# A trunk of one retention layer and one attention layer on one core: norm row spread by products with ones, sample rows handled last, program order in the output projection

## The chip, the cores and the metric

The kernel runs on one NeuronCore of one Trainium2 chip, as one program for the whole inference step. The metric is device time in microseconds (us) of one execution, the median of three runs. Names of engines: PE is the tensor engine (PEld its weight loads), DVE the vector engine, ACT the scalar engine, POOL the GpSimd engine, SP the engine that only issues transfers; ACT issues transfers too.

## The reference, cut to what matters

Two layers, first retention, then sliding-window attention, on 1024 prompt tokens and on 8 sample ("decode") tokens, each of 1024 features. All numbers are fp32.

```python
def rmsnorm(x, g):
    y = x * rsqrt(mean(x * x, -1) + EPS); return y * g

# layer 0, retention: h = rmsnorm(x, norm_ret); q, k, v, gate = split(h @ w_in_ret)
#   o = chunkwise recurrent retention, also the new state;  o = rmsnorm(o, ret_out_norm) * silu(gate)
#   x = x + o @ w_out_ret
# layer 1, attention: h = rmsnorm(x, norm_swa); q, k, v, gate = split(h @ w_in_swa)
#   q = rmsnorm(q, q_norm); k = rmsnorm(k, k_norm)          # per head of 64
#   p = softmax over a 128-token window, with one sink column per head and a linear bias
#   o = (p @ v) * silu(gate);  x = x + o @ w_out_swa
```

Outputs are both token sets after the trunk, the retention states and the last window of keys and values. The sample tokens attend to 128 cached keys each.

## The kernel before, in words

PE works nearly all the time on products in which each fp32 operand is split into a high and a low part, and three products (high by high, high by low, low by high) are summed in PSUM. So almost every operand passes through a pair of operations first: a copy to the high part on ACT, and a subtraction that gives the low part on DVE or POOL. The order of PE's instructions is the order in which the code issues them, throughout. On the other engines there are two regimes. In the first stage (everything inside the stack `se`) and in the first part of the attention layer (`sk`), `manual_schedule` names ACT, DVE, POOL and SP too, and they run in program order. After `sk.close()` (attention proper and the output projection), a scheduler in the compiler orders these four engines by its own estimates.

**The start (lines 382 to 502 and 861 to 898).** The prompt comes in chunks of 128 tokens, `X[0]` to `X[7]`; `X[8]` is the 8 sample rows. `xload(c)` loads a chunk on SP's queue. `sq(c)` makes the sum of squares on ACT (line 431), `pw(c)` the power -1/2 of the mean on POOL (lines 435 and 120), `sc(c)` multiplies the chunk by that and by the norm row `gb` on DVE (line 440), `TR(c, b)` transposes the eight 128 by 128 blocks of it on PE (line 105) into two PSUM banks, and `hi` and `lo` (457 and 461) split the transposed blocks into the operands `xh` and `xl`. `gb` is the vector `norm_ret` on all 128 partitions: one transfer that reads the row 128 times, 512 KB, on ACT's queue (line 866). The sample rows are transposed into `p8` (tile `pd`), copied to `rdec`, and `dcols` (495 and 496) puts two of their columns behind each 256 token columns of `xh` and `xl`. `w_hi` and `w_lo` (221 and 226) split the weights. The first products are plain ones (line 544, in slots of 24 matmuls); the first slot reads the columns of chunk 0, chunk 2 and the sample rows, and the third slot begins with the transposes of chunk 1. Between the first two slots' weight splits (on POOL) and those transposes lie `pw(1)` on POOL and `sc(1)` on DVE.

**The attention's last turns (lines 2360 to 2395).** 64 units (head pair by chunk) go through scores (`att_s`, 1988 to 1992), normalisation (`att_r`, 1999 and 2000), transposes (`att_x`) and the product with values (`att_o`, 2022; `att_out`, 2036). For the last head pair, `att_out` writes the operand of the output projection itself: the high part on ACT (line 2044), the low part on DVE (line 2045), into `SA`. From unit 58 on, `fill` mixes in products of the output projection.

**The output projection (`so_all`, from line 2189).** 24 products (8 feature tiles by 3 token ranges) of 24 matmuls each (lines 1660 to 1662) rotate over three PSUM tiles. `finish` adds the residual on DVE (2232), `so_y` transposes on DVE (2164), and four transfers on ACT's queue write the result; residual tiles `xr` (two buffers) are loaded on SP's queue (2220, 2222) when one is free; `so_ahead` loads and splits the next weight slot (1646, 1649, 1650). The third token range has the sample columns as well.

**The decode attention,** mixed into these products. `dec_scores` first computes the factor `r16` of the sample queries (tile `r`: lines 2068 to 2070 and 2072 on DVE, and the power on POOL, line 120 of `rsq`), then scores, softmax over 16 rows by 1032 columns (2081 to 2097, with an exponential on ACT, 2092). `dec_pt` transposes the result and builds `PTd` (ACT, 2109) and the masked `M8` (DVE, 2110; tile `pm`). `dec_o` multiplies with the values (2122, 2124), copies to `god` (tile `gdec`, ACT, 2128), multiplies by the gate (2130) and writes the sample columns of `SA`, high (2131) and low (2132).

Of the kernel before, what the change touches and what calls it, by code (L numbers as in the profile page):

```python
# [7 lines left out]
F32 = mybir.dt.float32  # L8
F32R = mybir.dt.float32r
AF = mybir.ActivationFunctionType  # L10
ALU = mybir.AluOpType
# [3 lines left out]
D = 1024  # L15
NP = 1024
# [8 lines left out]
HD = 64  # L25
# [45 lines left out]
def _trunk(ctx, tc, nc, a):  # L71
# [343 lines left out]
    X, SS, PO = {}, {}, {}  # L415

    def xload(c):
        if c in (0, 1, 2, 3):
            X[c] = xq.tile([128, D], F32, tag="xq", bufs=4, name="xq")
        elif c == 7:  # L420
            X[c] = raw_tile()
        else:
            X[c] = sp.tile([128, D], F32, tag="u", bufs=3, name="u")
        if c == 8:
            X[c] = X[c][0:ND, :]
        nc.sync.dma_start(out=X[c], in_=x_sample[:, 0, :] if c == 8 else x_prompt[0, c * 128:c * 128 + 128, :])
# [436 lines left out]
    for r in range(2):  # L863
        pool.memset(oneh[:, r, r:r + 1], 1.0)
    pool.memset(rdec32, 0.0)
    nc.scalar.dma_start(out=gb, in_=norm_ret[0].partition_broadcast(128))
    nc.scalar.dma_start(out=ident, in_=a["c1"][:, 0:128])
    act(warm, warm, AF.Silu)
    for c in (0, 8, 2):
        xload(c)  # L870
# [5 lines left out]
        raw_load(k0, r, nc.sync)  # L876
    for c in (4, 6, 7):
        xload(c)
    for c in (8, 0, 2):
        sq(c)  # L880
        pw(c)
    sc(8)
    p8 = vdp.tile([128, 8, ND], F32, tag="vd", name="pd8")
    for k in range(8):
        tr(p8[:, k, :], X[8][:, k * 128:k * 128 + 128], ident[:ND, :ND])
    sc(0)
    TR(0, 1)
    dve.tensor_copy(rdec, p8)
    sc(2)
    TR(2, 2)  # L890
    dcols(0, B11)
    dcols(0, B21)
    for c, name in ((0, "A11"), (2, "A12")):
        for j in range(2):
            hi(c, j)
            lo(c, j)
        w_hi(q0, name, 0)
        w_lo(q0, name, 0, pool)
    ev.sort(key=lambda e: e[:2])
    for n, s in enumerate(slots):  # L900
        while pes and pes[0][0] <= s.t:
# [1160 lines left out]

    dd = {}

    def dec_scores():

        rr = rbc[0:16, NP:NT]
        nc.vector.tensor_tensor(r16, ms16, rr, ALU.mult)
        nc.vector.tensor_tensor(r16, r16, rr, ALU.mult)
        nc.vector.tensor_scalar(r16, r16, 1.0 / HD, EPS, ALU.mult, ALU.add)  # L2070
        rsq(r16, r16, 8)
        nc.vector.tensor_tensor(r16, r16, rr, ALU.mult)
        ddec = atp.tile([16, 129], F32, tag="s", name="ddec", bufs=6)
        nc.sync.dma_start(out=ddec, in_=a["c2"][0:16, c2w() - 129:])
        S16 = rbc[0:16, :].rearrange("p (b s) -> p b s", b=8)
        for hf in range(2):
            psc = scp.tile([128, 512], F32, tag="sc", name="sc")
            for i in range(4):
                b = 4 * hf + i
                mm(psc[:16, i * 128:i * 128 + 128], Qd[:, :, b], kcT["t"][:, b, :], start=True, stop=True)  # L2080
            nc.vector.tensor_tensor(S16[:, 4 * hf:4 * hf + 4, 0:128], psc[:16, :].rearrange("p (b s) -> p b s", b=4),
                                    r16[:, 4 * hf:4 * hf + 4].unsqueeze(2).broadcast_to([16, 4, 128]), ALU.mult)
        pn = trp.tile([128, 512], F32, name="tr")
        for b in range(8):
            mm(pn[:16, b:b + 1], Qd[:, :, b], kdT[:, b:b + 1], start=True, stop=True)
        nc.vector.tensor_tensor(S16[:, :, 128], pn[:16, 0:8], r16, ALU.mult)
        nc.vector.tensor_tensor(S16, S16, ddec.unsqueeze(1).broadcast_to([16, 8, 129]), ALU.add)
        nc.vector.tensor_reduce(m16, S16, mybir.AxisListType.X, ALU.max)
        nc.vector.tensor_scalar(m16, m16, skc, None, ALU.max)
        nc.vector.tensor_tensor(S16, S16, m16.unsqueeze(2).broadcast_to([16, 8, 129]), ALU.subtract)  # L2090
        S16f = rbc[0:16, :]
        nc.scalar.activation(S16f, S16f, AF.Exp)
        nc.scalar.activation(e16, m16, AF.Exp, scale=-1.0, bias=skc)
        nc.vector.tensor_reduce(t16, S16, mybir.AxisListType.X, ALU.add)
        nc.vector.tensor_tensor(t16, t16, e16, ALU.add)
        nc.vector.reciprocal(t16, t16)
        nc.vector.tensor_tensor(S16, S16, t16.unsqueeze(2).broadcast_to([16, 8, 129]), ALU.mult)
        dd["S"] = S16
# [253 lines left out]
    for m in range(0, NU, 2):  # L2352
        if m == 50:
            so_ahead(1)
        if m == 56:
            drain(ps)
            so_ahead(2)
        if m == 58:
            so_ahead(3)
            src = out  # L2360
        reloads(m)
        sc_(m + L)
        fill(src, W)
        sc_(m + L + 1)
        fill(src, W)
        if m % 4 == 2:
            us = units[m - 2:m + 2]
            for u in us:
                until(G, (u.p, u.ti))
            att_o(us)  # L2370
        fill(src, 2 * W)
        for n_ in (2, 3):
            if m + n_ < NU:
                att_x(units[m + n_])
            fill(src, W)
        att_split()
        reloads(m)
    reloads(NU)
    fill(out, 6.0)
    assert not held & {4, 5}  # L2380
    dec_scores()
    dec_vload()
    fill(out, 14.0)
# [43 lines left out]
```

## Time and profile before

| quantity | us |
|---|---|
| median of three runs | 1290.34 (1289.12 to 1291.25) |
| the profiled execution's own time | 1292.0 |
| its span on the core | 1290.2 |
| PE busy in the span | 1263.0 (98%) |

The page gives the busy time of each engine, windows give it for stretches of the span together with the granted clock of PE (1.00 is full speed) and the transfers' rate, the list of waits says which instruction of which line released a waiting one, and the timeline lists instructions in order of time, with the idle time ahead of them in brackets. All times are counted from the span's start. What lies between span and time of the execution is 1.8 us here.

### The profile page before, as it was taken

To read this page: it belongs to the slowest core of one execution; us is meant where nothing else is said; L and a number is where in the kernel's file an instruction comes from. 1 tells how busy PE (TensorE), PEld (TensorE's weight loads), DVE (VectorE), ACT (ScalarE), POOL (GpSimd) and SP (SyncE) were. 2 spreads that over 40 slices of the span, in tenths; PEclk is the share of its full clock that TensorE was granted. 3 is DMA by queue.
4 is the path that set the end of the run, shared out by engine and by line. 5 is a ranking of instruction groups with operands and counts; after the bars stand their busy time and mean duration, and the time that the engine had idled before them with its cause. 6 is when DMAs were issued, how large, how long until landed. Compare 5 with 4: busy or idle time off the path is not lost.

```text
span 1290.2 us, 26727 instructions
## 1 busy us (share of the span) xinstructions
PE 1263.0 (98%) x9780; PEld 1210.0 (94%) x9780; DVE 778.8 (60%) x1512; ACT 647.7 (50%) x1570; POOL 730.6 (57%) x838
## 2 busy tenths in 40 slices
PE   6999999999999999999999999999999999998998
PEld 5999999999999999988889999999999999998988
DVE  5954656665575764476774656764667666765422
ACT  5533445454555554588771234545566655663010
POOL 5654444535359899798771457726465655654010
PEclk9999999999999999999999999999999999999989
DMA  6313867687668683556879855943031222237434
GB/s 227 108 54 120 252 186 233 182 253 216 189 208 229 189 243 103 184 173 204 264 209 258 234 188 159 276 118 103 19 114 50 66 67 67 66 111 241 85 75 86
DMA packets 245679, 206.68 MB, mean 160 GB/s; under 512 B 63992, under 2 KB 220532, under 8 KB 245532
## 3 DMA queue, kind: packets, MB, share of 16 engines
q1 hardware_dynamic: 189840, 170.61, 44.0%
q10 hardware_dynamic: 55708, 34.37, 9.1%
q8 instruction: 77, 1.26, 0.4%
q14 instruction: 54, 0.44, 0.1%
HBM read 135.41 MB, written 70.55 MB: 160 GB/s over the span
## 4 chain that ended last, share of the span: by engine, by line
PE 88%; DVE 4%; DMA 2%; ACT 2%; POOL 2%; issue 1%; SPq 0%; ACTq 0%; DVEq 0%; POOLq 0%
PE b L335 8%; PE b L336 8%; PE b L337 8%; PE S L1302 7%; PE pj L1660 6%; PE pj L1661 5%; PE pj L1662 5%; PE b L328 4%; PE b L329 4%; PE b L330 4%; PE tr L105 4%; PE o L2022 2%; PE b L544 1%; PE S L335 1%; PE S L336 1%
## 5 line engine op out<-in xcount | busy, mean ns | idle before, releaser
L335 PE MATMUL b<-xh,woh 128*128 128x258 f32 x784 | 223.2, 285 | 0.0
L337 PE MATMUL b<-xh,wol 128*128 128x258 f32 x784 | 221.7, 283 | 0.0
L336 PE MATMUL b<-xl,woh 128*128 128x258 f32 x784 | 221.6, 283 | 0.0
L1660 PE MATMUL pj<-SA,wh 128*128 128x384 f32 (+1 forms) x496 | 168.5, 340 | 2.2 <-DVE qs L1876 0.8
L1661 PE MATMUL pj<-SA,wh 128*128 128x384 f32 (+1 forms) x496 | 159.1, 321 | 2.8 <-DVE SA L2045 2.5
L1662 PE MATMUL pj<-SA,wl 128*128 128x384 f32 (+1 forms) x496 | 159.0, 321 | 0.0
L335 PEld LDWEIGHTS b<-xh,woh 128*128 128x128 f32 x784 | 148.0, 189 | 4.1 <-issue 4.1
L336 PEld LDWEIGHTS b<-xl,woh 128*128 128x128 f32 x784 | 148.7, 190 | 0.0
L337 PEld LDWEIGHTS b<-xh,wol 128*128 128x128 f32 x784 | 148.0, 189 | 0.0
L226 POOL TENSOR_TENSOR wol<-raw,woh 128x512 fp32r<-128x512 f32 x51 | 66.1, 1304 | 120.5 <-ACT woh L221 118.3
L328 PE MATMUL b<-woh,xh 128*128 128x256 f32 x448 | 126.6, 283 | 0.0
L329 PE MATMUL b<-wol,xh 128*128 128x256 f32 x448 | 126.0, 281 | 0.0
L330 PE MATMUL b<-woh,xl 128*128 128x256 f32 x448 | 125.6, 280 | 0.0
L2000 POOL TENSOR_TENSOR s<-s,sm 128x512 f32<-128x512 f32 x64 | 67.0, 1048 | 70.1 <-DVE sm L1999 58.5
L1660 PEld LDWEIGHTS pj<-SA,wh 128*128 128x128 f32 x496 | 93.6, 189 | 6.8 <-issue 2.6
L1661 PEld LDWEIGHTS pj<-SA,wh 128*128 128x128 f32 x496 | 94.0, 189 | 3.2 <-DVE SA L2045 2.8
L1650 POOL TENSOR_TENSOR wl<-wr,wh 128x512 fp32r<-128x512 f32 x40 | 51.3, 1296 | 77.4 <-ACT wh L1649 76.3
L1662 PEld LDWEIGHTS pj<-SA,wl 128*128 128x128 f32 x496 | 93.5, 188 | 0.0
L328 PEld LDWEIGHTS b<-woh,xh 128*128 128x128 f32 x448 | 84.3, 188 | 5.0 <-issue 2.9
L1992 ACT ACTIVATE s<-s,mx 128x257 f32<-128x257 f32 x128 | 64.2, 504 | 46.5 <-DVE mx L1990 41.4
L330 PEld LDWEIGHTS b<-woh,xl 128*128 128x128 f32 x448 | 84.3, 188 | 0.0
L329 PEld LDWEIGHTS b<-wol,xh 128*128 128x128 f32 x448 | 84.3, 188 | 0.0
(530 smaller groups left out, 3588.2 us busy)
## 6 DMA issues: line engine op xcount, KB each, us to landing
raw<-in_w_in_ret_dram ACTq DMA_DIRECT2D x44, 512.0 KB
st<-in_state_ret_dram SPq DMA_DIRECT2D x64, 256.0 KB
out_dram<-st SPq DMA_DIRECT2D x64, 256.0 KB
vb<-vscr SPq DMA_DIRECT2D x64, 128.0 KB
evp<-qks SPq DMA_DIRECT2D x32, 256.0 KB
evx<-vsc SPq DMA_DIRECT2D x32, 256.0 KB
wr<-in_w_in_swa_dram SPq DMA_DIRECT2D x32, 256.0 KB
evc<-gsc SPq DMA_DIRECT2D x16, 256.0 KB
```

The source lines that it names most:

```text
L226: eng.tensor_tensor(lo, src_of(s, name, sub), hi.bitcast(F32), SUB)
L328: mm(dst, xh, wh, start=a and i == 0, stop=False, skip_group_check=True)
L329: mm(dst, xh, wl, start=False, stop=False, skip_group_check=True)
L330: mm(dst, xl, wh, start=False, stop=z, skip_group_check=True)
L335: mm(dst, wh, xh, start=a, stop=False, **sg)
L336: mm(dst, wh, xl, start=False, stop=False, **sg)
L337: mm(dst, wl, xh, start=False, stop=z, **sg)
L1302: mm(box[0], s.op[f"A{i + 1}{j + 1}", 0][w][:, k, :], xs_[t][x[j]][:, k, :], start=(xs_ is XH and w == 0 and j + k == 0), stop=(xs_ is XL ...
L1660: mm(ps, hi[:, k, fs], xh[:, k, t0:t1], start=first and k == ks[0], stop=False)
L1661: mm(ps, hi[:, k, fs], xl[:, k, t0:t1], start=False, stop=False)
L1662: mm(ps, lo[:, k, fs], xh[:, k, t0:t1], start=False, stop=last and k == ks[-1])
L2000: nc.gpsimd.tensor_tensor(st[:, :, 0:256], st[:, :, 0:256], sm.unsqueeze(2).broadcast_to([128, 2, 256]), ALU.mult)
```

## The change

Three things change; the PE order is otherwise the same.

1. At the start, the norm row is loaded once (one row, 4 KB) into the buffer that chunk 3 takes later; two products of it with a row of ones (line 875 of the changed kernel) spread it over the 128 partitions into PSUM, and two DVE copies (888) bring it to `gb`. Chunk 3's load then has to wait until these products have read the row. Chunk 0 and chunk 2 are normalised and transposed first, and the sample rows after them; their columns for the first slot are taken straight from `p8`, and `rdec` is written later. The first weight split stands before chunk 2's high parts, the second behind its low parts.
2. The decode query factor leaves `dec_scores` for `dec_norm`: its first three DVE operations and the power are issued at unit 58, the last multiply before the projection's `fill(out, 6.0)`.
3. From `dec_scores` on, ACT, DVE, POOL and SP run in program order to the end.

```diff
     def xload(c):
-        if c in (0, 1, 2, 3):
+        if c in (0, 1, 2):
...
-        else:
+        elif c != 3:
...
-    nc.scalar.dma_start(out=gb, in_=norm_ret[0].partition_broadcast(128))
+    X[3] = xq.tile([128, D], F32, tag="xq", bufs=4, name="xq")
+    grow = X[3][0:1, :]
+    nc.scalar.dma_start(out=grow, in_=norm_ret[0:1, :])
     nc.scalar.dma_start(out=ident, in_=a["c1"][:, 0:128])
+    row1 = dcp.tile([1, 128], F32, name="row1")
+    dve.memset(row1, 1.0)
+    bank_of = {}
+    for j in range(2):
+        bank_of[0, j] = bank(0, j)
+        mm(bank_of[0, j], row1, grow[:, 512 * j:512 * j + 512], start=True, stop=True)
...
-    for c in (8, 0, 2):
+    for j in range(2):
+        dve.tensor_copy(gb[:, 512 * j:512 * j + 512], bank_of[0, j])
+    for c in (0, 2, 8):
         sq(c)
         pw(c)
+    sc(0)
+    TR(0, 1)
+    sc(2)
+    TR(2, 2)
     sc(8)
     p8 = vdp.tile([128, 8, ND], F32, tag="vd", name="pd8")
...
+    for j in range(2):
+        hi(0, j)
+        lo(0, j)
+    w_hi(q0, "A11", 0)
+    for j in range(2):
+        hi(2, j)
+    dcols(0, B11, p8[:, 0:4, 0:2])
+    dcols(0, B21, p8[:, 4:8, 0:2])
     dve.tensor_copy(rdec, p8)
...
+    for j in range(2):
+        lo(2, j)
+    w_lo(q0, "A11", 0, pool)
+    w_hi(q0, "A12", 0)
+    w_lo(q0, "A12", 0, pool)
...
+    def dec_norm(part):
+        rr = rbc[0:16, NP:NT]
+        if part == 0:
+            nc.vector.tensor_tensor(r16, ms16, rr, ALU.mult)
+            nc.vector.tensor_tensor(r16, r16, rr, ALU.mult)
+            nc.vector.tensor_scalar(r16, r16, 1.0 / HD, EPS, ALU.mult, ALU.add)
+            rsq(r16, r16, 8)
+        else:
+            nc.vector.tensor_tensor(r16, r16, rr, ALU.mult)
...
         if m == 58:
+            dec_norm(0)
...
     reloads(NU)
+    dec_norm(1)
     fill(out, 6.0)
     assert not held & {4, 5}
+    ctx.enter_context(tc.manual_schedule(engines={ET.Activation, ET.DVE, ET.Pool, ET.SP}))
     dec_scores()
```

The start on DVE, before: `u` holds the sample rows, `xq` a chunk, `ss` the power, `pd` the transposed sample rows, `b` a PSUM bank of a transposed chunk.

```order
L440 SCALAR_TENSOR_TENSOR u<-u,ss,gb 8x1024
L440 SCALAR_TENSOR_TENSOR xq<-xq,ss,gb 128x1024
L888 COPY rdec<-pd_174 128x8x8
L440 SCALAR_TENSOR_TENSOR xq<-xq,ss,gb 128x1024
L495 CAST xh<-rdec 128x4x2
L496 TENSOR_TENSOR xl<-rdec,xh 128x4x2
L495 CAST xh<-rdec 128x4x2
L496 TENSOR_TENSOR xl<-rdec,xh 128x4x2
L461 TENSOR_TENSOR xl<-b_184,xh 128x4x128
```

And now, on the same engine from the memset of the row of ones on (`row`):

```order
L871 MEMSET row_137 1x128
L888 COPY gb<-b_139 128x512
L888 COPY gb<-b_141 128x512
L440 SCALAR_TENSOR_TENSOR xq<-xq,ss,gb 128x1024 x2
L440 SCALAR_TENSOR_TENSOR u<-u,ss,gb 8x1024
L461 TENSOR_TENSOR xl<-b_182,xh 128x4x128
L461 TENSOR_TENSOR xl<-b_183,xh 128x4x128
L495 CAST xh<-pd_204 128x4x2
L496 TENSOR_TENSOR xl<-pd_204,xh 128x4x2
```

Both chunks now stand ahead of the sample rows, and the first chunk's low parts ahead of the sample columns; two copies stand ahead of all of it.

The attention's last turns on DVE, before: `s` are scores, `mx` and `sm` their row maxima and sums, `ot` the gated output, `SA` the projection's operand, `r` the decode query factor.

```order
L1988 SCALAR_TENSOR_TENSOR s<-sc,rq,ndp 128x256
L2068 TENSOR_TENSOR r_11355<-ms_11354,rbc 16x8
L1990 TENSOR_REDUCE mx<-s 128x2
L1999 RECIPROCAL sm<-sm 128x2
L2036 SCALAR_TENSOR_TENSOR ot<-o,gt 128x384
L2036 SCALAR_TENSOR_TENSOR ot<-o,gt 128x128
L2069 TENSOR_TENSOR r_11355<-r_11355,rbc 16x8
L2070 TENSOR_SCALAR r_11355<-r_11355 16x8
L1999 RECIPROCAL sm<-sm 128x2
L2072 TENSOR_TENSOR r_11355<-r_11355,rbc 16x8
L2045 TENSOR_TENSOR SA<-ot,SA 128x384
```

And now at the same place (lines 2083 to 2085 and 2088 are the factor's, 2051 is the gated output, 2060 the operand's low part):

```order
L2084 TENSOR_TENSOR r_11363<-r_11363,rbc 16x8
L2003 SCALAR_TENSOR_TENSOR s<-sc,rq,ndp 128x256
L2085 TENSOR_SCALAR r_11363<-r_11363 16x8
L2003 SCALAR_TENSOR_TENSOR s<-sc,rq,ndp 128x256
L2005 TENSOR_REDUCE mx<-s 128x2
L2014 RECIPROCAL sm<-sm 128x2
L2003 SCALAR_TENSOR_TENSOR s<-sc,rq,ndp 128x256
L2088 TENSOR_TENSOR r_11363<-r_11363,rbc 16x8
L2051 SCALAR_TENSOR_TENSOR ot<-o,gt 128x384
L2005 TENSOR_REDUCE mx<-s 128x2
L2014 RECIPROCAL sm<-sm 128x2
L2060 TENSOR_TENSOR SA<-ot,SA 128x384
```

The factor's first three operations have moved up among the scores; its last multiply stands ahead of the gated output instead of between it and `SA`.

The decode attention's end on DVE, before: `sq` is a product with its residual, `ptf` its transpose, `pm` the masked `M8`, `gdec` the gated decode output.

```order
L2232 TENSOR_TENSOR sq<-pj,xr_15968 128x384
L2164 STREAM_TRANSPOSE ptf<-sq 128x384
L2232 TENSOR_TENSOR sq<-pj,xr_16016 128x384
L2164 STREAM_TRANSPOSE ptf<-sq 128x384
L2110 TENSOR_TENSOR pm_15992<-tr,ident 8x128
L2130 TENSOR_TENSOR gdec<-gdec 128x64
L2232 TENSOR_TENSOR sq<-pm,xr_16068 128x384
L2131 CAST SA<-gdec 128x8x8
L2164 STREAM_TRANSPOSE ptf<-sq 128x384
L2132 TENSOR_TENSOR SA<-gdec,SA 128x8x8
```

And now:

```order
L2129 TENSOR_TENSOR pm_16002<-tr,ident 8x128
L2251 TENSOR_TENSOR sq<-pj,xr_15978 128x384
L2183 STREAM_TRANSPOSE ptf<-sq 128x384
L2149 TENSOR_TENSOR gdec<-gdec 128x64
L2150 CAST SA<-gdec 128x8x8
L2151 TENSOR_TENSOR SA<-gdec,SA 128x8x8
L2251 TENSOR_TENSOR sq<-pj,xr_16026 128x384
```

`pm` has moved ahead of two products' ends, and the operations that write the sample columns of `SA` now follow each other.

More of the change, by code (lines that the diff above doesn't have):

```diff
@@ L885, in _trunk @@
         tr(p8[:, k, :], X[8][:, k * 128:k * 128 + 128], ident[:ND, :ND])
-    sc(0)
-    TR(0, 1)
-    dve.tensor_copy(rdec, p8)
[L889 to L898, printed above, removed]
+    for j in range(2):
[6 more added lines that the diff above has]
+    dcols(0, B21, p8[:, 4:8, 0:2])
+    dve.tensor_copy(rdec, p8)
+    for j in range(2):
[3 more added lines that the diff above has]
+    w_lo(q0, "A12", 0, pool)
     ev.sort(key=lambda e: e[:2])
@@ L2063, in _trunk @@
     dd = {}
-    def dec_scores():
[L2067 to L2072, printed above, removed]
+    def dec_norm(part):
[7 more added lines that the diff above has]
+            nc.vector.tensor_tensor(r16, r16, rr, ALU.mult)
+    def dec_scores():
         ddec = atp.tile([16, 129], F32, tag="s", name="ddec", bufs=6)
```

## Prediction

> **What bounds the kernel now.** I read the busy times first, then who PE waited for, then the clock in windows around the longest waits, then the timeline there.
>
> ```profile
> PE 1263.0 (98%) x9780; PEld 1210.0 (94%) x9780; DVE 778.8 (60%) x1512; ACT 647.7 (50%) x1570; POOL 730.6 (57%) x838
> ```
>
> ```profile
> PE pd L105 <- DVE u L440: 9.9, 1, 9.9
> PE pj L1661 <- DVE SA L2045: 2.5, 1, 2.5
> ...
> PE o L2122 <- DVE pm L2110: 1.5, 1, 1.5
> ...
> PE pj L1660 <- ACT SA L2044: 0.7, 1, 0.7
> ```
>
> PE is the bound; no other engine passes 60%. As the change leaves PE's products alone, it can only win where PE waits or runs slowly. The list of PE's waits has its large entries at the start (9.9 us until the first transposes) and at the end of the program, and those at the end are exactly the places that the change reorders. The windows show that the end costs more than its waits; the column behind POOL's is PE's granted clock:
>
> ```profile
> 22.10:25.50 3.40, 2.17 (x20) 1.99 (x19) 3.40 (x4) 1.51 (x4) 2.91 (x4) 1.00 0.16 43
> 1175.80:1179.20 3.40, 0.66 (x3) 0.19 (x1) 1.70 (x5) 0.82 (x3) 3.01 (x3) 1.00 1.08 358
> 1179.20:1182.70 3.50, 3.07 (x11) 2.98 (x12) 1.52 (x3) 0.60 (x1) 0.00 (x0) 0.51 0.20 55
> 1182.70:1230.40 47.70, 47.70 (x320) 46.48 (x319) 19.53 (x33) 4.16 (x8) 0.00 (x0) 1.00 0.47 101
> 1230.40:1233.90 3.50, 1.98 (x15) 1.57 (x14) 1.30 (x3) 0.00 (x0) 0.00 (x0) 0.99 0.46 86
> 1233.90:1240.70 6.80, 6.80 (x25) 6.80 (x25) 0.23 (x1) 0.76 (x4) 0.00 (x0) 0.50 0.38 99
> 1240.70:1285.00 44.30, 43.32 (x307) 42.32 (x306) 11.62 (x26) 4.06 (x11) 5.04 (x4) 1.00 0.42 81
> ```
>
> After the stretch with 0.66 us of PE work in 3.4 the clock is 0.51 for 3.5 us, and after the one with 1.98 in 3.5 it is 0.50 for 6.8 us. A stretch with 2.17 in 3.4, near the start, had no such sequel.
>
> **The start.** The transfers' rate and the timeline:
>
> ```profile
> 0.00:4.10 4.10, 0.00 (x0) 0.00 (x0) 0.11 (x3) 1.49 (x2) 0.72 (x8) 1.00 0.49 154
> 4.10:5.90 1.80, 0.00 (x0) 0.00 (x0) 0.00 (x0) 0.00 (x0) 0.00 (x0) 1.00 0.88 293
> ```
>
> ```profile
> 6.53 1.05 ACT L431 ACTIVATE junk<-u 8x1024 f32<-8x1024 f32 x1 [3.38 <-DMA u<-in_x_sample_dram]
> ...
> 7.71 1.06 ACT L431 ACTIVATE junk<-xq 128x1024 f32<-128x1024 f32 x1
> ...
> 10.63 1.28 DVE L440 SCALAR_TENSOR_TENSOR xq<-xq,ss,gb 128x1024 f32<-128x1024 f32 x1 [0.74 <-POOL ss L120]
> ...
> 13.98 1.48 PEld L105 LDWEIGHTS b<-ident,xq 128*128 128x128 f32 x8 [0.44 <-DVE xq L440]
> ...
> 16.23 1.66 ACT L221 ACTIVATE woh<-raw 128x512 fp32r<-128x512 f32 x3
> ...
> 16.93 3.80 POOL L226 TENSOR_TENSOR wol<-raw,woh 128x512 fp32r<-128x512 f32 x3 [0.47 <-ACT woh L221]
> ...
> 21.66 2.30 DVE L440 SCALAR_TENSOR_TENSOR xq<-xq,ss,gb 128x1024 f32<-128x1024 f32 x1 [3.40 <-POOL ss L120]
> ...
> 24.07 0.86 PEld L105 LDWEIGHTS b<-ident,xq 128*128 128x128 f32 x8 [1.41 <-issue]
> ```
>
> ACT waits for the sample rows until 6.53, because the 512 KB of the spread norm row travel with chunk 0. In order of time the chain is: sums of squares of the sample rows, then chunks 0 and 2, transposes of chunk 2 at 13.98, its high parts, the second weight split at 16.23, three POOL subtractions (3.80 from 16.93), the power and scaling of chunk 1 (21.66), its transposes at 24.07. From there PE is full. So the gain is what 24.07 moves, and that hangs on the transposes of chunk 2.
>
> Removed: the 512 KB. By 4.1 us the transfers had moved 4.10 x 154 = 631 KB, by 5.9 another 527. Now chunk 0 (524 KB), the identity (66) and the 4 KB row make 594, so chunk 0 is there by about 4.1; chunk 2 is 524 more, so by 5.9. From the start of a chunk's sum of squares to its scaling took 7.71 to 10.63, 2.92 us. Chunk 2 is then scaled at 5.9 + 2.92 = 8.8 (chunk 0 from 7.0 to 8.3, so DVE is free), and transposed at 8.8 + 1.28 = 10.1 instead of 13.98: 3.8 us. Added: two products and two copies that have about 3 us between the row's arrival and 7.0, and the wait of chunk 3's load for those products on SP's queue, ahead of weight loads that ACT reads only after 20 us; I cost both at nothing. The sample rows' scaling and transposes now follow chunk 2's on DVE and PE (1.3 and 1 us) and would come to lie on the path of the first slot, not of the POOL chain; as PE idles ahead of 24.07 anyway (1.41), they hide there. If the loads came no sooner, only the sample rows' place would be saved, 7.71 - 6.53 = 1.2 us. A faster step than 2.92 (POOL's power is held up by DVE in it) could give 4.6. I take **3.8**, from 1.2 to 4.6.
>
> **The attention's last turns.**
>
> ```profile
> 1173.52 0.88 DVE L2068 TENSOR_TENSOR r<-ms,rbc 16x8 f32<-16x8 f32 x1
> ...
> 1178.12 0.99 DVE L2072 TENSOR_TENSOR r<-r,rbc 16x8 f32<-16x8 f32 x1 [1.67 <-POOL r L120]
> 1179.04 0.54 DVE L2045 TENSOR_TENSOR SA<-ot,SA 128x384 fp32r<-128x384 f32 x1
> ```
>
> ```profile
> 1167.18 5.21 POOL L1650 TENSOR_TENSOR wl<-wr,wh 128x512 fp32r<-128x512 f32 x4 [2.59 <-ACT wh L1649]
> ...
> 1176.47 1.62 POOL L120 TENSOR_TENSOR r<-r,mhalf 16x8 f32<-16x8 f32 x1 [0.28 <-DVE sm L1999]
> 1178.07 1.03 POOL L2000 TENSOR_TENSOR s<-s,sm 128x512 f32<-128x512 f32 x1
> ```
>
> ```profile
> 1176.11 0.51 ACT L2044 ACTIVATE SA<-ot 128x384 fp32r<-128x384 f32 x1
> ```
>
> ```profile
> 1176.67 0.44 PE L1660 MATMUL pj<-SA,wh 128*128 128x384 f32 x1 [0.65 <-ACT SA L2044]
> 1179.63 0.69 PE L1661 MATMUL pj<-SA,wh 128*128 128x384 f32 x1 [2.52 <-DVE SA L2045]
> ```
>
> ```profile
> 1209.64 0.15 DVE L2086 TENSOR_TENSOR rbc<-tr,r 16x8 f32<-16x8 f32 x1
> ```
>
> PE stands still until 1179.63 because the low part of `SA` queues on DVE behind the factor's last multiply, which waits for POOL's power (to 1178.09). Now the power stands on POOL behind the four weight subtractions and one normalisation: 1172.4 + 1.03 = 1173.4 (1174.1 if that normalisation waits for DVE), plus 1.0 to 1.62: 1175.1 at the earliest reading, 1175.7 at the latest. The multiply still stands on DVE ahead of the gated output, so it still gates: 0.15 to 0.99 for it, then the gated output (about 0.5), the high part 0.51, the low part 0.54: PE restarts between 1176.9 and 1178.2, and up to 0.8 later if the three earlier operations are held up among the scores. That is 0.6 to 2.7 gained; I take **1.8**. A 16x8 multiply lasted 0.88 and 0.99 here while POOL was busy, so the row already carries that cost. [...]
>
> Clock: the gap shrinks to about 1 to 1.5 us of 3.4, so PE's work there is near the 2.17 that had no sequel. From 1179.63 to 1182.70 half a clock cost 3.07 / 2 = **1.5**; I count it as won.
>
> **The decode attention in the projection.**
>
> ```profile
> 1226.09 0.28 ACT L2109 ACTIVATE pm<-tr 128x128 f32<-128x128 f32 x1 [11.00 <-PE tr L105]
> ```
>
> ```profile
> 1232.11 0.24 DVE L2110 TENSOR_TENSOR pm<-tr,ident 8x128 f32<-8x128 f32 x1
> ```
>
> ```profile
> 1232.88 2.73 PE L2124 MATMUL o<-pm,wr 128*128 128x16 f32 x16
> ```
>
> `M8` reads what `PTd` reads (ACT had it at 1226.09), but stood on DVE behind two products' ends until 1232.11. It now stands ahead of both, so PE's 1.5 us go: **1.5**. With the gap the slow clock should go too: 6.8 us at half cost up to 3.4; the 16-column products until about 1235.6 may not follow the clock, without them it is 2.5. I take **3.1**.
>
> ```profile
> 1242.78 0.18 DVE L2131 CAST SA<-gdec 128x64 fp32r<-128x64 f32 x1
> ```
>
> ```profile
> 1243.02 0.39 PE L1660 MATMUL pj<-SA,wh 128*128 128x264 f32 x1 [0.75 <-DVE SA L2131]
> ```
>
> The sample columns likewise: their writing waited behind a product's end; now it follows the gate at once. PE idled 44.30 - 43.32 = 1.0 us in that stretch: **1.0**, from 0.8 to 1.4.
>
> What program order adds:
>
> ```profile
> 1213.73 0.54 DVE L2232 TENSOR_TENSOR sq<-pj,xr 128x384 f32<-128x384 f32 x1
> ...
> 1218.88 1.22 DVE L2097 TENSOR_TENSOR rbc<-rbc,t 16x1032 f32<-16x1032 f32 x1
> ```
>
> The product end at 1213.73 now waits for the whole softmax, which starts only after the factor's work and now ends at about 1217.8 in place of 1220.1 (an estimate: two such ends and their transposes no longer stand ahead of it), some 4 us late. A product is 24 matmuls of 47.70 / 320 = 0.149, 3.6 us, and with three PSUM tiles its bank is needed two products later, 7.2 us: hidden by 3 us, and each us beyond that would be PE's. The residual load queues behind that product's end on SP and has the same slack. The last weight slot's two loads are now issued on SP behind the second residual of the last token range; the slot is split only when PE has left it, some 6 us after the sample columns:
>
> ```profile
> 1249.55 0.63 ACT L1649 ACTIVATE wh<-wr 128x512 fp32r<-128x512 f32 x1 [13.11 <-PE pj L1661]
> ```
>
> I cost all this at nothing.
>
> **Sum:** 3.8 + 1.8 + 1.5 + 1.5 + 3.1 + 1.0 = 12.7 us. Against the profiled execution (1292.0, span 1290.2) that is 1279.3, span 1277.5; the median of the runs shown is 1290.34, which gives **1277.6**.
>
> **Rivals.**
> - *The decode products slow the clock by themselves.* Sixteen products of 16 columns stay, 2.73 us of thin work, and half of the slow stretch came after PE was busy again. For: the second half of the 6.8 us. Against: the gap is gone. Price: 3.4 us at half, 1.7, up to all 3.1: 1279.3 to 1280.7. Chance 0.17.
> - *The attention's wait is only moved.* The multiply waits for a power that POOL reaches late, ahead of the gated output. Price 1.8 + 1.5: 1280.9. Chance 0.15.
> - *The slow stretches do not come from these gaps.* Both then stay, as windows of the clock that fall so anyway: 1.5 + 3.1 lost, 1282.2. Against: they follow the only two long gaps after 25 us. Chance 0.06. [...]
> - *The loads come no sooner*, and the start gives 1.2: 1280.2. Chance 0.07.
> - *The start's gain is eaten before the end* by a stage that some load paces: 3.8 lost, 1281.4. PE's list has no wait for a transfer. Chance 0.02.
> - *Slower:* program order chains each product's end to its predecessor's transpose, whose buffer waits for transfers that ACT issues in order. It decides once that chain lasts longer than the three PSUM tiles, over 7.2 us a product. If each of the 18 products after the switch then waited as long as the 1.5 us of `dec_o`, 27 us would be lost against 12.7: 1304.6. Against: DVE is busy 11.62 of 44.30 us there. Chance 0.04, of which 0.01 just cancels the gain.
>
> My forecast keeps 0.49. About 0.2%, 2.6 us, is what a measurement of this kernel can tell from no change: faster 0.96, same 0.01, slower 0.03. The range reaches from all upper bounds (4.6, 2.7, 3.4 and 1.4 in place of what I took, 1275.2) to the rival with both slow stretches: 1275.0 to 1282.3.
>
> **What would show it.** Right: chunk 0's sum of squares on ACT near 4.1, transposes of chunk 1 near 20.3; waits for the low part of `SA` near 1 us; no wait of `dec_o` for `pm`; no window with a clock near 0.5 between 25 and 1280. Wrong: a slow window behind the decode products, PE waiting for a residual or PSUM tile in the projection, or a first slot that starts no sooner.

## The result and the profile after

The changed kernel took 1284.91 us (median of 7 runs, 1283.13 to 1286.32), the kernel before, on the same chip, 1290.98 (1289.12 to 1294.99). The ratio is 0.9946, 95% interval 0.9934 to 0.9957: a gain of 5.6 to 8.5 us, where 12.7 had been forecast. The time lies above the range's upper end of 1282.3. The profiled execution took 1284.27 with a span of 1282.4 (before 1292.0 and 1290.2), so 7.7 and 7.8 us.

The page's busy times hardly moved:

```profile
PE 1263.4 (99%) x9784; PEld 1209.2 (94%) x9784; DVE 780.0 (61%) x1515; ACT 647.9 (51%) x1570; POOL 731.6 (57%) x838
```

By this count the gain is idle time of PE; what the clock gives or takes lies within the busy time. The list of PE's waits after (who waited, for whom; total, count and the longest in us):

```profile
PE b L875 <- DMA xq<-in_norm_ret_dram: 2.9, 1, 2.9
PE tr L105 <- DVE on L1082: 2.7, 2, 1.8
PE b L105 <- DVE xq L440: 2.3, 1, 2.3
PE pj L1675 <- ACT SA L2059: 1.8, 1, 1.8
PE tr L105 <- ACT ptf L2191: 1.1, 1, 1.1
```

In place of the 9.9 us until the first transposes stand 2.9 for the norm row and 2.3 for chunk 0, with the two products that spread the row between them. The 2.5 for the low part of `SA` and the 1.5 of `dec_o` are gone. The wait for the high part of `SA` has grown from 0.7 to 1.8, and new are one of 1.8 in the retention layer (`on`, the normalised output) and one of 1.1 for `ptf` near the end. The windows after, cut at the borders of the clock's steps (columns as before: busy time of PE, PEld, DVE, ACT, POOL, then PE's granted clock):

```profile
11.65:15.05 3.40, 2.29 (x22) 1.99 (x21) 3.33 (x10) 3.40 (x7) 2.94 (x3) 1.00 1.10 370
15.05:18.45 3.40, 3.40 (x19) 3.40 (x18) 1.86 (x4) 0.55 (x2) 3.10 (x4) 0.50 1.02 405
...
1172.18:1175.59 3.41, 2.47 (x23) 1.99 (x19) 3.11 (x7) 1.10 (x4) 3.07 (x3) 1.00 1.08 385
1175.59:1179.00 3.41, 2.41 (x14) 2.08 (x15) 2.76 (x8) 2.21 (x6) 1.90 (x2) 1.00 0.56 183
1226.79:1230.20 3.41, 3.41 (x26) 3.16 (x25) 0.03 (x1) 0.77 (x4) 0.00 (x0) 1.00 0.02 3
1230.20:1233.61 3.41, 3.41 (x13) 3.41 (x12) 1.65 (x5) 0.00 (x0) 0.00 (x0) 0.50 0.30 63
```

The half-speed stretch behind the attention is gone; the one behind the decode products is half as long (3.4 us in place of 6.8), and the start has one that it did not have. The 1.00 of windows ahead of 11.65 us (15.3 before) is no measurement: the record of the clock begins there, with a change, for in both kernels a transpose of 128 columns takes 0.42 us ahead of that point and 0.27 behind it.

**A ledger.** PE runs the same products in the same order in both kernels, so the start of one product before minus its start after is the gain up to there:

| PE's product | before | after | gained so far |
|---|---|---|---|
| transposes of chunk 1 | 24.10 | 21.36 | 2.74 |
| first retention output's transposes | 542.31 | 541.72 | 0.59 |
| a product late in the attention | 1168.36 | 1166.99 | 1.37 |
| second product with the last `SA` | 1179.64 | 1177.04 | 2.60 |
| the same, when the clock is full again | 1182.6 | 1178.6 | 4.0 |
| first decode product with the values | 1232.50 | 1226.93 | 5.57 |
| first product with the sample columns | 1243.03 | 1234.98 | 8.05 (the next 8.54) |
| behind the last `ptf` of the sample rows | 1258.56 | 1251.40 | 7.16 |

The last row stays to PE's end; 0.65 more come behind it. A gain that drifts over hundreds of microseconds says little: the kernel with the decode norm split alone (below), whose code is the same as before up to unit 58, stands 2.1 us behind before at 1100. Steps at one product that other profiles repeat are what counts. So the change won up to 2.7 us at the start and had 0.6 of it left at 542 us, 1.6 having gone in one step there; it won 2.6 in the attention's last turns and 4.6 around the decode attention, and lost 1.4 at the end.

### The profile page after: what moved, and what is told of

It reads as the page before. It is cut to its first block, busy times and chain, and to the rows that moved or that the text cites. A ratio compares the mean times of both kernels' runs of the same rounds, so it can differ in the third digit from the quotient of the medians.

```text
span 1282.4 us, 26734 instructions
## 1 busy us (share of the span) xinstructions
PE 1263.4 (99%) x9784; PEld 1209.2 (94%) x9784; DVE 780.0 (61%) x1515; ACT 647.9 (51%) x1570; POOL 731.6 (57%) x838
```

## The experiments

My theory on seeing this: three separate leaks, namely a new wait that the row of ones brings into the retention layer, a decode clock that falls for the thin products alone, and transfers that program order puts ahead of ACT's copies. The rival: the parts interact, so that a part done alone would not give its share.

**One part at a time.** Each is the kernel before with one of the three parts: the start; the split of the decode norm; one line for program order.

```diff
-    nc.scalar.dma_start(out=gb, in_=norm_ret[0].partition_broadcast(128))
+    nc.scalar.dma_start(out=grow, in_=norm_ret[0:1, :])
...
+    row1 = dcp.tile([1, 128], F32, name="row1")
...
```

```diff
         if m == 58:
+            dec_norm(0)
...
     reloads(NU)
+    dec_norm(1)
```

```diff
+    ctx.enter_context(tc.manual_schedule(engines={ET.Activation, ET.DVE, ET.Pool, ET.SP}))
     dec_scores()
```

> The kernel before with the change at the start alone. Theory (the start gives less than forecast, and a later stage takes back part of it): transposes of chunk 1 near 21.4 us as in the changed kernel, 2.7 us sooner than before, a granted clock near 0.5 between about 15 and 18.5 us, and at the end of the retention stage (700 us) not more than 1.4 us of it left; time 1 to 1.5 us under before, ratio 0.9989 to 0.9992. Rival (the loss in the retention stage belonged to the one profiled execution): 2.7 us at the end, ratio 0.9979.

> The kernel before with only the decode query factor split off and begun at unit 58. Theory (its multiply still gates the gated output, but the wait is short enough for the clock to stay up): PE waits 1.8 + 0.2 us for SA in place of 0.7 + 2.5, no clock of 0.5 behind it; 2.6 us in all, ratio 0.998. Rival (with the scheduler still on, the decode operations behind it move as well and eat it): ratio 0.999 to 1.0005.

> The kernel before with only program order from the decode scores on. Theory (program order by itself puts the factor's operations behind the writing of SA, so the split adds nothing to it): the wait for SA falls to about 0.7 + 0.1 us, no slow clock behind it (3.9 us), dec_o's wait of 1.5 and the 1.0 us for the sample columns go, one slow window of two goes (1.7), and 1.4 us are lost again at the transfers' waits near the end; 6.7 us, ratio 0.9948. Rival (the attention's wait needs the split): 2.8 us, ratio 0.9978.

| part alone | ratio (95%) | median | before beside it |
|---|---|---|---|
| start | 0.9991 (0.9982 to 1.0) | 1289.9 | 1292.18 |
| decode norm split | 0.9979 (0.9971 to 0.9987) | 1289.44 | 1292.18 |
| program order | 0.9969 (0.9959 to 0.9979) | 1288.39 | 1292.18 |

The parts give 0.9, 2.1 and 3.1 thousandths, 6.1 in all; the whole gives 5.4 (and 6.8 when run again, below). They add up within the intervals, so interaction is not what is missing. The start is the part that failed: about 1.2 us of 3.8 (0 to 2.3 by its interval).

PE's waits with program order alone, and with the split alone:

```profile
PE pj L1661 <- DVE SA L2045: 2.5, 1, 2.5
...
PE tr L105 <- ACT ptf L2172: 1.2, 1, 1.2
```

```profile
PE pj L1660 <- ACT SA L2044: 1.8, 1, 1.8
...
PE o L2126 <- DVE pm L2114: 1.5, 1, 1.5
```

The first has the old wait for `SA` and the new one for `ptf`, the second the reverse: the shorter attention wait belongs to the split, the loss at the end to program order. I had expected program order to shorten the attention's wait by itself, for 6.7 us in all; it does not, and its 4.0 us lie nearer to the rival's 2.8.

**Where the start's gain goes.** The row of ones was a tile of its own, 512 bytes on each partition. This kernel takes it from `gb`, which is still empty then:

```diff
-    row1 = dcp.tile([1, 128], F32, name="row1")
+    row1 = gb[0:1, 512:640]
```

> The changed kernel with the row of ones kept in a part of gb that is not yet written, in place of a tile of its own of 512 bytes per partition. In the built program of the changed kernel ACT's first square of the retention waits for PE's product 4296, twelve behind the one it reads; here, as in the kernel before, for the one it reads. Theory (the new tile moves the later tiles by 512 bytes, so that one lands on operands that PE still reads): PE's wait for on near 542 us falls from 1.79 to 0.2 us, 1.6 us less at the end, ratio 0.9933. Rival (the wait is that of a chain on ACT and DVE, and would come later): the wait stays or moves behind it, ratio 0.9946.

The timeline at the first retention output, before, after, and with this edit:

```profile
539.43 0.60 ACT L1055 ACTIVATE on<-po 128x512 f32<-128x512 f32 x1
...
542.31 0.66 PE L105 MATMUL tr<-ident,on 128*128 128x128 f32 x4 [0.20 <-DVE on L1067]
```

```profile
539.29 0.60 ACT L1070 ACTIVATE on<-po 128x512 f32<-128x512 f32 x1 [1.10 <-PE S L1034]
...
541.72 0.66 PE L105 MATMUL tr<-ident,on 128*128 128x128 f32 x4 [1.79 <-DVE on L1082]
```

```profile
539.80 0.65 PE L105 MATMUL tr<-ident,on 128*128 128x128 f32 x4 [0.20 <-DVE on L1082]
540.73 0.68 PE L779 MATMUL tr<-evp 128*128 128x128 f32 x4 [0.28 <-PE tr L105]
...
546.50 0.68 PE L779 MATMUL tr<-evp 128*128 128x128 f32 x4 [0.73 <-DVE kl L791]
```

After, ACT's square into `on` stands ready for `po` but waits 1.10 for another product (`S`, line 1034), and PE waits 1.79 in place of 0.20. The product that it waits for is twelve behind the last that writes `po`; with the edit it waits for the one that it reads again. So the new tile shifted the tiles behind it until `on` lay on operands that PE was still reading, and the wait is undone by giving the 512 bytes back. That the tile makes the wait is shown: all seven profiles that have it lose 1.6 us at this product, and the others do not. That `on` came to lie on operands still being read is argued from the later product. That giving it back pays is not shown: the next waits (0.28, then 0.73 for `kl`) take most of it, and the time was 1285.08, ratio 0.9936 (0.9921 to 0.9951), not told apart from the changed kernel. The kernel with the start alone has the same wait of 1.79.

**Idle products at the start.** Between 12.2 and 13.9 us PE has only the sample rows' transposes, 0.66 us, and from 15.05 on the clock is half. This kernel gives it work that nothing reads:

```diff
+    busy = bank(1, 0)
+    for j in range(4):
+        mm(busy[:, 0:128], row1, row1, start=True, stop=True)
+    def dummy(n):
+        for _ in range(n):
+            mm(bank_of[0, 1][:, 0:128], ident, ident, start=True, stop=True)
...
     TR(2, 2)
+    dummy(3)
...
+    dummy(5)
```

> The changed kernel with idle PE time at the start filled with work that nothing reads: four products of a row of ones with itself behind the two that spread the norm row, three of the identity with itself ahead of the sample rows' transposes, five behind them. Theory (the start is slowed by a granted clock of 0.5, which follows PE's pauses there): no clock near 0.5 between 12 and 25 us, transposes of chunk 1 at 19.7 to 20.2 us in place of 21.4 to 22.4, and 1.2 to 2 us less at the end; ratio to before 0.9931 to 0.9937. Rival (the first slots wait for the scaling of chunk 1, not for PE): transposes at 21 or later, ratio 0.9946.

The transposes of chunk 1, after, with the start alone, and with the idle products:

```profile
21.36 1.04 PE L105 MATMUL b<-ident,xq 128*128 128x128 f32 x8
```

```profile
22.42 1.04 PE L105 MATMUL b<-ident,xq 128*128 128x128 f32 x8
```

```profile
20.24 1.03 PE L105 MATMUL b<-ident,xq 128*128 128x128 f32 x8
```

With the idle products they come at 20.24. That this is near the 20.3 forecast is in part luck: chunk 1 is scaled by 19.37 there, and PE comes last here too. In the eight other profiles with this start and no idle products in it they come between 20.65 and 22.42, and only the one at 20.65 waits for the scaled chunk:

```profile
20.65 1.06 PE L105 MATMUL b<-ident,xq 128*128 128x128 f32 x8 [0.99 <-DVE xq L440]
```

In the rest PE comes last. Only the changed kernel's first profile has a half window recorded there, but the others run at half rate as well, ahead of their clock's record. Five of them have 6 to 8 matmuls in each us from 15 to 17, and 11 from 19 to 20. With the start alone eight products of 258 columns take 1.92 us, and a little later 1.12:

```profile
17.42 1.92 PE L544 MATMUL b<-xl,woh 128*128 128x258 f32 x8
...
20.50 1.12 PE L544 MATMUL b<-xh,wol 128*128 128x258 f32 x8
```

In the seven other profiles the record begins, with full speed, at 20.0, 18.5, 17.8, 17.5, 16.8, 16.5 and 12.1 us, and the gain at these transposes is, in the same order, 1.68, 1.99, 2.57, 2.78, 3.05, 3.32 and 3.45 us. So how much of the start's gain arrives goes with the moment at which PE's clock becomes full (3.5 us sooner, from 20.0 to 16.5, gives 1.6 us). In the kernel before this was 15.3, ahead of all first products (from 15.79); the changed start begins these near 14.

But the kernel took 1287.18, ratio 0.9957 (0.9942 to 0.9971), no better. Between 814 and 967 us PE falls 3.6 us back against before, 2.7 of it from 890 to 900, with a wait of ACT of 1.2 us for a weight load at 891 and of PE of 0.9 for `qs`, and then a slow window at 895.68. The order of the instructions there is the same, and why that load comes late is open.

**Thin products mixed with wide ones.** In `dec_o`, three matmuls of the projection after each of the eight 16-column products, and fewer ahead of them:

```diff
             mm(po[:, b, :], vc[:, b, :], PTd[:, b, :], start=False, stop=(b == 7))
+            fill(out, 0.1)
...
-    fill(out, 4.0)
+    fill(out, 1.5)
```

> The changed kernel with three full products between each two of the decode products of 16 columns, which begin 2.5 us of fill sooner. Theory (products of 16 columns leave PE's array so thinly used that the clock falls, without any gap): no clock near 0.5 behind the decode products, 1.7 us under the changed kernel, ratio to before 0.9933. Rival (a window falls slow there whatever PE does): a clock near 0.5 there as in the changed kernel, ratio 0.9946.

The windows at the decode products with this edit:

```profile
1226.82:1230.23 3.41, 3.41 (x23) 3.04 (x22) 0.52 (x1) 0.00 (x0) 0.00 (x0) 1.00 0.50 106
1230.23:1233.65 3.42, 3.42 (x25) 3.42 (x24) 1.14 (x2) 0.00 (x0) 0.00 (x0) 1.00 0.11 16
```

PE is busy 3.41 of 3.41 here and after alike, but with wide products between the thin ones the clock stays full. So the clock does not go by "busy" alone. Of the four kernels that mix the products none has a half window behind them. Of the changed kernel's two profiles and the four others that start from it and leave the products as they are, three have one. In two of the other three the thin products lie across two windows; in the third, the one with the row of ones in `gb`, all lie in one (1229.26 to 1231.22, in 1229.19 to 1232.60), and no half speed follows. That mixing helps is therefore likely, from few profiles, and not shown. The time was 1284.41, ratio 0.9937 (0.9924 to 0.995): in the profiled run the 1.7 us were spent again by a half window in the attention (below).

**The attention's multiply on POOL.** The last multiply of the query factor leaves DVE, where it stands ahead of the gated output:

```diff
-            nc.vector.tensor_tensor(r16, r16, rr, ALU.mult)
+            nc.gpsimd.tensor_tensor(r16, r16, rr, ALU.mult)
```

> The changed kernel with the last multiply of the decode query factor on POOL, behind the power there, in place of DVE. Theory (the multiply on DVE waits for the power ahead of the gated output and holds it up): PE's wait for SA falls from 1.8 to about 0.6 us, and 1.2 us less at the end; ratio to before 0.9937. Rival (PE then waits for the gate or the attention's product instead): the wait stays above 1.4 us, ratio 0.9946.

The timeline there, after and with the edit:

```profile
1172.72 1.62 POOL L120 TENSOR_TENSOR r<-r,mhalf 16x8 f32<-16x8 f32 x1
1174.38 0.99 DVE L2088 TENSOR_TENSOR r<-r,rbc 16x8 f32<-16x8 f32 x1 [0.30 <-POOL r L120]
1175.30 0.54 DVE L2051 SCALAR_TENSOR_TENSOR ot<-o,gt 128x384 f32<-128x384 f32 x1
1176.44 0.45 PE L1675 MATMUL pj<-SA,wh 128*128 128x384 f32 x1 [1.79 <-ACT SA L2059]
```

```profile
1174.69 2.02 POOL L2015 TENSOR_TENSOR s<-s,sm 128x512 f32<-128x512 f32 x2
1175.36 1.77 DVE L2060 TENSOR_TENSOR SA<-ot,SA 128x384 fp32r<-128x384 f32 x1
1175.38 0.44 PE L1675 MATMUL pj<-SA,wh 128*128 128x384 f32 x1 [0.63 <-ACT SA L2059]
1177.18 0.59 PE L1676 MATMUL pj<-SA,wh 128*128 128x384 f32 x1 [1.36 <-DVE SA L2060]
```

The first wait falls to 0.63 as it should, but the low part of `SA` now lies across two normalisations of POOL and takes 1.77 us, where after it takes 0.55, and PE waits 1.36 for that. Two waits of 2.0 in all stand against 1.9, and the time is the same: 1284.7, ratio 0.9936 (0.9923 to 0.9949). That the normalisations are what lengthens it is not shown: after, one of POOL ran beside it as well, from 1176.58 on.

**The last copy ahead of the transfers.** In `so_y`, the sample rows' transpose, copy and transfer move ahead of the loop of four transfers:

```diff
+            if ti == 2:
...
             for q in range(4):
                 f0 = ft * 128 + 32 * q
                 nc.scalar.dma_start(...)
-            if ti == 2:
...
```

> The changed kernel with the sample rows' transpose, copy and transfer ahead of the four transfers of the prompt rows, in the code that ends a product. Theory (in program order the copy on ACT stands behind four transfers that wait for free buffers, and PE's next transpose waits for the copy): PE's wait of 1.1 us for ptf near 1251 us goes; ratio 0.9937. Rival (the buffers themselves come free too late): the wait is only moved, ratio 0.9946 or above.

The timeline of ACT's issues (ACTq), its copy and PE's next transpose after, and that transpose with the edit:

```profile
1247.43 3.59 ACTq L2186 DMA_DIRECT2D out_dram<-ptf  x4
1251.07 0.27 ACT L2191 ACTIVATE ptf<-tr 8x128 f32<-8x128 f32 x1 [4.06 <-DMA out_dram<-ptf]
1251.39 0.27 PE L105 MATMUL tr<-ident,sq 128*8 128x128 f32 x1 [1.12 <-ACT ptf L2191]
```

```profile
1249.94 0.27 PE L105 MATMUL tr<-ident,sq 128*8 128x128 f32 x1
```

After, ACT issues four transfers, which takes it 3.59 us, and only then makes the copy that frees the bank for PE. Of the 3.59, 1.9 lie between the first issue and the second. With the copy first, PE's wait is gone and 1.45 us are kept to the end of the profiled run; over 6 runs the median was 1283.94, ratio 0.9928 (0.9914 to 0.9942), not told apart from the changed kernel's second measurement, 0.9932 (below).

**All four, and idle products for the attention's gap.** First the four edits together; then the same with seven idle products of 384 columns, that nothing reads, while PE waits for `SA`; beside them the changed kernel again; last the same without the idle products at the start:

```diff
+            if (ft, ti) == (0, 0):
+                idle = trp.tile([128, 512], F32, name="tr")
+                for _ in range(7):
+                    mm(idle[:, :n], so_slots[0][0][:, 0, 0:128], A_hi[:, 0, t0:t1], start=True, stop=True)
```

> The changed kernel with four of the earlier edits together: idle products at the start, the row of ones inside gb, the decode products mixed with full ones, and the sample rows' copy ahead of the transfers. Theory (each removes its own loss from PE's path: 1.1 us at the start, 0.3 at the retention, 1.4 at the decode products where the clock falls there, 1.4 at ptf): ratio to before 0.9910 to 0.9920, and no slow clock but perhaps one behind the wait for SA. Rival (the losses cover each other): 0.9928, as with the ptf edit alone.

> The kernel of the last run, with seven products of 384 columns that nothing reads ahead of the first product that waits for SA, 1.2 us of work in a wait of 1.8. Theory (the clock of a 3.4 us window is halved when the window before it, on the clock's own grid, held less than about 1.5 us of wide products, so the wait for SA halves it or not by where it falls on the grid): the wait shrinks to about 0.6 us, no slow window behind it wherever the grid lies, no cost; 0 to 1.7 us under the last run, ratio 0.9905 to 0.9915. Rival (only PE's wait counts, not what fills it): as the last run.

> The changed kernel itself once more, beside the two others on one chip. Theory (the slow windows fall by chance of the grid): the same waits as in its first profile (1.8 us for SA, 1.79 for on, 1.1 to 1.5 for ptf), but slow windows at other places or in another number; ratio 0.994 to 0.9952. Rival (slow windows belong to places in the program): the same two, behind the start and behind the decode products.

> The changed kernel without idle products at the start, but with the row of ones inside gb, the decode products mixed with full ones, the sample rows' copy ahead of the transfers, and seven idle wide products in the wait for SA. Theory (the idle products at the start cost more than they give, since three kernels with them lost 2 us between 814 and 967 us; the other edits each keep their gain): no slow clock between 25 and 1280 us but at most one near 970, no wait at ptf, SA's wait about 0.6 us; ratio to before 0.9910 to 0.9922. Rival (the edits at the end cover each other): 0.9928, as with the ptf edit alone.

| kernel | ratio (95%) | median | before beside it |
|---|---|---|---|
| four edits | 0.9953 (0.9937 to 0.9968) | 1286.93 | 1292.81 |
| and idle products in the gap | 0.9946 (0.9931 to 0.9961) | 1286.24 | 1292.81 |
| the changed kernel again | 0.9932 (0.9918 to 0.9945) | 1283.93 | 1292.81 |
| without those at the start | 0.9922 (0.9908 to 0.9935) | 1281.3 | 1292.34 |

The first two missed what I expected of them, and part of the cause is that two of the edits collide. The row of ones lies in the second half of `gb` here, four of the idle products read it, and the copy that fills that half waits for them (the four edits):

```profile
7.76 0.69 DVE L896 COPY gb<-b 128x512 f32<-128x512 f32 x1 [2.72 <-PE b L878]
```

So chunk 0 is scaled from 8.67, where the idle products by themselves had it from 7.01, and the transposes of chunk 1 come at 22.57 and 22.14 in these two kernels in place of 20.24. They are no test of idle products at the start. What all three kernels with them share is a loss of 1.2 to 3.0 us near 895, whose cause is open. Without them the median is the lowest of all, and the clock stays full from 12.1 to 1278 us. Its interval overlaps those of the changed kernel, so that it is better still is likely and not shown. The windows across the attention's gap, for the changed kernel again and for this last one:

```profile
1173.62:1177.03 3.41, 1.62 (x10) 1.31 (x8) 3.11 (x8) 1.68 (x6) 2.18 (x3) 1.00 1.09 376
1177.03:1180.44 3.41, 3.38 (x12) 2.91 (x13) 1.75 (x5) 1.63 (x5) 2.31 (x2) 0.50 0.30 93
...
1231.65:1235.06 3.41, 3.41 (x13) 3.41 (x12) 1.70 (x5) 0.28 (x2) 0.00 (x0) 0.50 0.21 51
```

```profile
1173.30:1176.71 3.41, 2.68 (x15) 2.11 (x13) 3.10 (x8) 2.13 (x7) 2.18 (x3) 1.00 1.09 363
1176.71:1180.12 3.41, 3.41 (x22) 3.34 (x23) 1.33 (x4) 1.19 (x5) 1.86 (x2) 1.00 0.60 173
```

The same kernel, run again, has a half window in the attention that its first profile did not have.

## Why the prediction was wrong

The direction and the places were right, and a bit over half of the size came.

- **The start, 3.8 forecast, 2.74 measured at its end and about 0.6 kept.** The step that failed: "From there PE is full. So the gain is what 24.07 moves". Two things were wrong with it. First, another bound took over. The timeline after:

```profile
4.74 1.06 ACT L431 ACTIVATE junk<-xq 128x1024 f32<-128x1024 f32 x1 [1.51 <-DMA xq<-in_x_prompt_dram]
6.25 0.56 POOL L120 TENSOR_TENSOR ss<-ss,mhalf 128x1 f32<-128x1 f32 x1
6.66 0.69 DVE L888 COPY gb<-b 128x512 f32<-128x512 f32 x1 [1.02 <-PE b L875]
7.57 1.28 DVE L440 SCALAR_TENSOR_TENSOR xq<-xq,ss,gb 128x1024 f32<-128x1024 f32 x1 [0.22 <-ACT junk L431]
12.11 5.31 POOL L226 TENSOR_TENSOR wol<-raw,woh 128x512 fp32r<-128x512 f32 x4 [0.86 <-ACT woh L221]
18.35 1.29 DVE L440 SCALAR_TENSOR_TENSOR xq<-xq,ss,gb 128x1024 f32<-128x1024 f32 x1 [1.53 <-POOL ss L120]
```

  POOL's first subtraction begins 3.1 us sooner (12.11 against 15.17), the fourth ends 3.3 sooner (17.42 against 20.73), and chunk 1 is scaled by 19.64; but PE, at half clock until 18.5, reaches the transposes only at 21.36. The forecast had PE's first two slots at full rate, as they were before; in the profiles above PE and its clock, not the chain through POOL, come last at these transposes in all but one. Chunk 0 was there at 4.74, not 4.1; its power was ready at 6.81, but the spread row's second copy ended at 7.35 and the scaling began at 7.57, so the row, costed at nothing, held it up by about 0.6 us. POOL's step ahead of the power did last longer beside DVE's scaling, 1.00 and 1.29 us at 8.95 and 10.68 before, where it took 0.19 at 20.81 with DVE idle. Second, 1.6 us of the gain were lost at 540 us to a tile that had moved, a cost that stands in no list of instructions, and 0.5 between 300 and 400 us for no cause that is known. The rival that the gain is eaten later had 0.02; its mechanism (a load that paces a stage) is not what happened first here.
- **The attention, 1.8 + 1.5 forecast, 2.6 measured.** The two waits of 0.65 and 2.52 became 1.79 and 0.15, so 1.2 of 1.8; the multiply still gates the gated output, as its row at 1174.38 shows. The half clock behind it was gone in the profiled run, which gave 1.4 of 1.5; in the second profile of the same kernel it was back. Over the eleven profiles with the split this stage gains 2.6 in the six without half speed behind the gap (two of them with the gap filled) and 1.0 to 1.3 in the five with it. So whether the 1.5 comes hangs on where the gap falls on the clock's grid (two windows with 2.47 and 2.41 us of work in this run, one with 1.62 in the second profile), and that it came in this run is luck. One slip in the sum: from 1173.4 the power's earliest end is 1174.4, not 1175.1, so that the upper bound of 2.7 was too low by 0.7.
- **The decode attention, 1.5 + 3.1 + 1.0 forecast, 4.6 measured.** The wait for `pm` went (1.6 from 1182 to the first product), and the sample columns' wait too. The clock gave 1.7 (half of the 3.4 us of slow stretch that went) of 3.1, and about 1.3 is left for the sample columns. In this profile the rival that the thin products slow it by themselves (0.17) was right, and at its lower price; a slow window behind them was one of the forecast's own signs of being wrong. It is not always so: in the four profiles that have program order, leave these products as they are and show no half speed behind them, the same stage gains 6.2 us.
- **Program order, costed at nothing, cost 1.4.** I had looked at DVE, SP and the PSUM tiles, and followed ACT's issues of transfers only in the rival that would have cost 27 us. The wait is of that kind, but comes once.

In sum, for the profiled run against the forecast: -3.2 at the start, -0.7 in the attention, -1.0 at the decode products and -1.4 at the end, and +0.8 and +0.65 that came unforecast between 542 and 1167 us and behind PE's last product. 12.7 - 4.9 = 7.8.

## What to carry to other kernels

An earlier start of the next stage was a gain here only as far as the engine that runs that stage could use it (PE's clock was half until 18.48 us): look at its clock and its idle time just ahead, not at the chain that used to release it alone. A new small tile of 512 bytes made a wait of 1.79 us at 541.72 by moving the tiles behind it, so borrow a buffer that is still empty, and compare what the first instructions of later stages wait for. When edits that work alone are put together, look for a buffer that two of them use. When a scheduler's order is replaced by program order, read each queue for a copy that stands behind a transfer's issue, ACT's as well.

## What was not expected of the hardware

**The clock's windows.** The half-speed stretches begin on a grid of 3.41 us steps that goes on where the clock does not change: before, it is full from 15.30, where the record begins, to 1179.24, which is 341 steps of 3.413, and the next half window is 16 steps on, at 1233.86; after, 356 steps lie between 15.06 and 1230.21. For the attention's gap, PE's busy time in the poorest such window was 0.62 us before, 0.61 with the start alone, and 1.41 to 1.70 in six profiles with a half window behind it; it was 2.41 or more in those without, except for two kernels with idle products at the start, at 1.62 and 1.65. Elsewhere busy time does not decide: windows with 2.38 (at 892.27, idle products), 2.41 (894.65, gap filled) and 2.54 us (968.36, program order alone) were followed by half speed too. All three hold products of 2 columns. If PE's time in products of 25 columns and fewer is left out (all others have 128 or more), the fourteen profiles agree: of the windows at full speed that the record covers, up to the last 7 us, all eight with at most 1.46 us of wider products were followed by half speed, and none with 1.88 or more; between 1.62 and 1.85 both occur.

The same gap of some 1.8 us falls into one window or is shared by two: in the changed kernel's first profile it is shared (2.47 and 2.41 us of work, no half speed), in the second it is not (1.62, then 3.4 us at half, and the stage gains 1.3 us in place of 2.6). The clock's rise at the start lies on the same grid; in five profiles, the one before among them, the window ahead of it held transposes alone, 2.7 to 3.4 us of them.

It takes no idle window for half speed to follow: a window with 1.62 us of work in it (from 1173.62 in the second profile) had 0.50 behind it, and so had one in which PE was busy throughout (3.41 us from 1226.79 in the first), 1.96 us of it with 16-column products:

```profile
1227.34 1.96 PE L2143 MATMUL o<-pm,wr 128*128 128x16 f32 x16
```

**Transfers' issue.** After, SP's issue of the `evp` transfer at 536.04 took 1.95 us, and 0.41 before. It ran beside a fetch of 16 KB of instructions. Of SP's 56 issues in that profile that overlap such a fetch, 23% took over 0.9 us, of the 703 others 1.4%. In all eleven profiles with the new start this issue lies beside such a fetch and takes 1.1 to 2.1 us; in the three without it there is none, and it takes 0.40. It may be a part of the waits that follow when the 512 bytes are given back, but no run here separates cause from coincidence.
